# Seven products of halves in place of eight for the gate products of a feed-forward part

## The chip, the core and the metric

One NeuronCore of a Trainium2 chip runs the whole program in one launch. The metric is the time of one execution on the device, in microseconds, as the median of several runs. PE is TensorE (PEld its weight loads), DVE is VectorE, ACT is ScalarE, POOL is GpSimd, and SP issues the DMAs.

## The reference

The input is 512 tokens of width 1024 in float32. Two blocks of a network follow. The second has two layers, and each layer has two feed-forward parts, one ahead of and one behind a token mixer:

```python
def swiglu(x, w_gate, w_up, w_down):
    return (jax.nn.silu(x @ w_gate) * (x @ w_up)) @ w_down
...
for l in range(DEPTH_2):
    h = h + 0.5 * swiglu(rmsnorm_2(h, ffn1_norm[l]), ffn1_w_gate[l], ffn1_w_up[l], ffn1_w_down[l])
    ...
    h = h + 0.5 * swiglu(rmsnorm_2(h, ffn2_norm[l]), ffn2_w_gate[l], ffn2_w_up[l], ffn2_w_down[l])
    gate = jax.nn.sigmoid(rmsnorm_2(h, ple_norm[l]) @ ple_w_gate[l])
    h = h + (p[l] @ ple_w_proj[l]) * gate
```

Here `x` is 512 x 1024, `w_gate` and `w_up` are 1024 x 2816 and `w_down` is 2816 x 1024. The change touches these four feed-forward parts alone.

## The kernel before, in words

Activations lie transposed, features on the 128 partitions and the 512 tokens along the free axis, so a vector of width 1024 is eight tiles of 128 x 512 (`h[k]`, `xh[k]`, `xl[k]`). A float32 product is made of three passes: each operand is split into a high part (ScalarE copies it into the narrower matmul type, L327) and a remainder (VectorE subtracts, L328), and `acc` (L384) issues high x low, low x high and high x high into one PSUM bank.

Weights come in units of 128 x 1024 (four k-tiles of 256 columns, 512 KB). `wunit` (L351) loads a unit on SP's queue into one of three `raw` buffers, and `split` makes `wh` and `wl`, three buffers each. `proj_a` takes 256 columns of a weight at a time: two banks, and for each unit and each half of 128 columns, twelve matmuls of 512 columns. After the last unit it calls the evacuation.

`swiglu_hidden` goes through the 2816 features in 11 pairs of tiles. For each pair it makes the gate products (`evac_g`: VectorE multiplies by the norm's row factors `x.R`, L1203, ScalarE takes Silu, L303) and the up products (`evac_u`: two VectorE multiplications, L1209 and L1210, and a split into `uh` and `ul`), 96 matmuls of 512 columns in all. Then `residual` multiplies all 22 tiles by `w_down`, 256 output columns at a time, and adds half of it to `h` (L1122); in doing so it calls `nxt.add`, which scales and splits `h` for the next part (L330, L331) and sums its squares (L468, L474).

`x.R` is not there when a part starts. `Next.start` puts two steps off by 5 and 8 us of matmul time: the sums over features (L509) and the chain of small VectorE instructions that makes the factors (L530, L521 to L525), and then their broadcast through DRAM (a transpose at L552, a copy at L554, two DMAs). For the first part `between` also rescales `h` by eight VectorE instructions (L1185). Results that come before the factors are held and evacuated after them.

Each engine's queue has an order that is fixed when the program is built. An instruction's rank is its place in the program text (`tc.cur_priority`), and on each engine the ready one of lowest rank goes next by modelled durations; buffers permitting, weights are split up to two units ahead. At run time no queue is reordered by the kernel.

```python
            self.push(self.proj_a(Wg, KD, [(mp * 256, 256)], x.hi, x.lo, evac_g))
            self.push(self.proj_a(Wu, KD, [(mp * 256, 256)], x.hi, x.lo, evac_u))
            self.drain()
        self.push(self.residual(Wd, KF, uh, ul, h, 0.5, nxt=nxt))
```

Of the kernel before, what the change touches and what calls it, by code (L numbers as in the profile page):

```python
# [10 lines left out]
F32 = mybir.dt.float32  # L11
F32R = mybir.dt.float32r
# [65 lines left out]
PASS = 0.2134 / 512  # L78
# [12 lines left out]
KEEP = 2  # L91
EARLY = 3
LATE = 5.0, 8.0
MA, MB, YN = 13, 13, 8
RAW, SPL = 3, 3
AHEAD, EVAC, BEHIND = 1000, -1000, 1000
# [28 lines left out]
class Net:  # L125
# [120 lines left out]
    def nm(self, s):  # L246
        self.n += 1
        return f"{s}{self.n}"

    PLACE = {"h": "H", "mix": "H", "xh": "X", "xl": "X", "mh": "X", "ml": "X", "uh": "U", "ul": "U",  # L250
             "qk": "W", "V": "W", "rc": "W", "hq": "Q", "yh": "Y", "yl": "Y", "oh": "Y", "ol": "Y", "gate": "G"}
    SHORT = ("R", "sq", "g", "u", "hd", "cv", "rows", "out", "lv", "rst", "rt")

    def S(self, name="s", dt=F32):

# [145 lines left out]
    def proj_b(self, W, K, segs, xh, xl, evac):  # L401

        ncol = sum(n for _, n in segs)
        shared = ncol <= 256
        if shared:
            ps = [self.wps() for _ in range(2)]
            ps = [ps[t // 2][:, (t % 2) * 256:(t % 2) * 256 + ncol] for t in range(NT)]
        else:
            ps = [self.wps()[:, :ncol] for _ in range(NT)]
        for k0, nk, (h, l) in self.units(W, K, segs):  # L410
            for t in range(NT):
                for k in range(nk):
# [5 lines left out]
                yield nk * 3 * ncol * PASS  # L418


    def columns(self, parts, dma):
# [30 lines left out]
    class Next:  # L452
# [23 lines left out]
        def start(self, long=True):  # L476
# [711 lines left out]


    def swiglu(self, h, norm, which, l, nxt):  # L1190
        with self.phase({"W": 8}, U=44):
            self.swiglu_hidden(h, norm(), which, l, nxt)

    def swiglu_hidden(self, h, x, which, l, nxt):
        nc, a = self.nc, self.a
        Wg, Wu, Wd = (a[f"{which}_w_{n}_2"][l] for n in ("gate", "up", "down"))
        uh, ul = [], []
        for mp in range(11):
            g = []

            def evac_g(j, p, g=g):
                t = self.S("g")
                nc.vector.tensor_tensor(t, p, x.R, op=OP.mult)  # L1203
                self.act("silu", t, t, AF.Silu)
                g.append(t)

            def evac_u(j, p, g=g):
                u = self.S("u")
                nc.vector.tensor_tensor(u, p, x.R, op=OP.mult)  # L1209
                nc.vector.tensor_tensor(u, u, g[j], op=OP.mult)  # L1210
                hi, lo = self.S("uh", F32R), self.S("ul", F32R)
                self.split(u, hi, lo)
                uh.append(hi)
                ul.append(lo)
            self.push(self.proj_a(Wg, KD, [(mp * 256, 256)], x.hi, x.lo, evac_g))
            self.push(self.proj_a(Wu, KD, [(mp * 256, 256)], x.hi, x.lo, evac_u))
            self.drain()
        self.push(self.residual(Wd, KF, uh, ul, h, 0.5, nxt=nxt))
        self.drain()

    def layer_consts(self):
        t = self.S("layer")
# [636 lines left out]
```

## Time and profile before

| | |
|---|---|
| runs | 3086.03 us median of 3 (3077.51 to 3086.58) |
| profiled execution | 3079.62 us, its span 3077.8 us |
| TensorE matmuls | 14805, 98% of the span busy |
| VectorE, ScalarE, GpSimd | 56%, 38%, 6% of the span busy |
| DMA | 318.69 MB, mean 104 GB/s |

A busy PE in the profile is an engine that has matmuls in flight; how fast it goes is read from the distance between the starts of neighbouring matmuls. PEclk is the granted clock in tenths of full speed.

### The profile page before, as it was taken

Reading aid. Unit: us, or ns where it says so; the run is one execution under the profiler, and the core shown is the slowest. Engines: PE = TensorE matmul, PEld = TensorE weight load, DVE = VectorE, ACT = ScalarE, POOL = GpSimd, SP = SyncE. Lnnn points to the kernel's source line nnn. Section 1 sums busy time; section 2 is a strip of 40 time slices with the busy share of each in tenths; the row PEclk is TensorE's granted clock in tenths of the full one; section 3 lists DMA queues with packets and bytes.
Section 4 is the critical chain, followed back from the end, with each engine's and each line's share of the span. In section 5 each row is a group of like instructions: output and inputs, shape, how many; then the busy total and the mean of one; then the engine's idle time right before and its main releaser. Section 6 shows DMA issues by size and latency. Waiting matters only on the chain.

```text
span 3077.8 us, 37929 instructions
## 1 busy us (share of the span) xinstructions
PE 3011.2 (98%) x14805; PEld 2501.5 (81%) x14805; DVE 1734.0 (56%) x2770; ACT 1159.8 (38%) x1794; POOL 171.1 (6%) x150
## 2 busy tenths in 40 slices
PE   9999999999999999999999999999999999999998
PEld 7778777888888888778888888888888788888888
DVE  5678666666454443587654433644435885644437
ACT  4454534444333322335333322433323353333225
POOL 0000221111000000112000000000000120000000
PEclk9999999999999999999999999999999999999999
DMA  6354324333233333333333333333333224333224
GB/s 206 119 130 131 100 82 129 93 102 96 93 93 110 96 95 97 97 91 86 109 100 96 96 96 99 100 103 96 93 96 106 84 69 126 93 98 98 91 95 152
DMA packets 309061, 318.69 MB, mean 104 GB/s; under 512 B 25230, under 2 KB 284005, under 8 KB 308882
## 3 DMA queue, kind: packets, MB, share of 16 engines
q1 hardware_dynamic: 303502, 307.24, 33.7%
q10 hardware_dynamic: 5380, 9.03, 1.0%
q8 instruction: 116, 1.90, 0.3%
q14 instruction: 63, 0.52, 0.1%
HBM read 289.77 MB, written 7.96 MB: 97 GB/s over the span
## 4 chain that ended last, share of the span: by engine, by line
PE 86%; DVE 7%; issue 3%; DMA 2%; ACT 2%; SPq 1%; POOL 1%; DVEq 0%; ACTq 0%; POOLq 0%
PE w L384 78%; DVE wl L328 2%; PE p L1419 1%; ACT wh L327 1%; PE p L762 1%; PE p L1512 1%; PE p L1580 1%; PE p L723 0%; PE p L769 0%; PE p L509 0%; DMA raw<-in_w_in_dram 0%; PE p L725 0%; PE p L1400 0%; DMA vec<-t5rows 0%; PE p L770 0%
## 5 line engine op out<-in xcount | busy, mean ns | idle before, releaser
L328 DVE TENSOR_TENSOR wl<-raw,wh 128x1024 fp32r<-128x1024 f32 (+3 forms) x524 | 634.6, 1211 | 874.2 <-ACT wh L327 863.1
L384 PE MATMUL w<-xl,wh 128*128 128x512 f32 (+1 forms) x2584 | 1000.9, 387 | 0.0
L384 PE MATMUL w<-xh,wh 128*128 128x512 f32 (+1 forms) x2584 | 998.5, 386 | 0.0
L384 PE MATMUL w<-xh,wl 128*128 128x512 f32 (+1 forms) x2584 | 998.1, 386 | 0.0
L327 ACT ACTIVATE wh<-raw 128x1024 fp32r<-128x1024 f32 (+3 forms) x524 | 537.8, 1026 | 1120.8 <-PE w L384 846.7
L384 PEld LDWEIGHTS w<-xl,wh 128*128 128x128 f32 x2584 | 487.0, 188 | 92.1 <-issue 0.6
L384 PEld LDWEIGHTS w<-xh,wh 128*128 128x128 f32 x2584 | 486.4, 188 | 92.1 <-issue 0.2
L384 PEld LDWEIGHTS w<-xh,wl 128*128 128x128 f32 x2584 | 486.7, 188 | 90.2
L384 PE MATMUL w<-uh,wl 128*128 128x512 f32 x880 | 342.3, 389 | 0.0
L384 PE MATMUL w<-ul,wh 128*128 128x512 f32 x880 | 342.3, 389 | 0.0
L384 PE MATMUL w<-uh,wh 128*128 128x512 f32 x880 | 342.3, 389 | 0.0
L384 PEld LDWEIGHTS w<-uh,wh 128*128 128x128 f32 x880 | 165.2, 188 | 34.4
L384 PEld LDWEIGHTS w<-ul,wh 128*128 128x128 f32 x880 | 165.2, 188 | 34.3
L384 PEld LDWEIGHTS w<-uh,wl 128*128 128x128 f32 x880 | 165.2, 188 | 34.2
L384 PE MATMUL w<-wh,xl 128*128 128x256 f32 (+2 forms) x480 | 141.2, 296 | 2.8 <-ACT wh L327 2.4
L384 PE MATMUL w<-wl,xh 128*128 128x256 f32 (+2 forms) x480 | 139.6, 291 | 0.0
L384 PE MATMUL w<-wh,xh 128*128 128x256 f32 (+2 forms) x480 | 137.8, 291 | 0.0
L1203 DVE TENSOR_TENSOR g<-w,R 128x512 f32<-128x512 f32 x88 | 60.5, 691 | 112.5 <-PE w L384 94.2
L327 ACT ACTIVATE uh<-u 128x512 fp32r<-128x512 f32 x88 | 55.7, 634 | 151.1 <-DVE u L1210 151.1
L303 ACT ACTIVATE g<-g 128x512 f32<-128x512 f32 (+1 forms) x112 | 65.8, 593 | 110.1 <-DVE g L1203 96.7
L384 PEld LDWEIGHTS w<-wh,xl 128*128 128x128 f32 x480 | 92.5, 193 | 7.3 <-ACT wh L327 2.6
L384 PEld LDWEIGHTS w<-wl,xh 128*128 128x128 f32 x480 | 92.8, 193 | 1.5 <-issue 0.7
(394 smaller groups left out, 3222.7 us busy)
## 6 DMA issues: line engine op xcount, KB each, us to landing
raw<-in_ffn_w_gate_dram SPq DMA_DIRECT2D x88, 512.0 KB, 3.8
raw<-in_ffn_w_up_dram SPq DMA_DIRECT2D x88, 512.0 KB, 3.8
raw<-in_ffn_w_down_dram SPq DMA_DIRECT2D x80, 512.0 KB, 3.5
raw<-in_w_in_dram SPq DMA_DIRECT2D x71, 512.0 KB, 3.9
raw<-in_w_up_dram SPq DMA_DIRECT2D x44, 512.0 KB, 3.5
raw<-in_w_gate_dram SPq DMA_DIRECT2D x32, 512.0 KB, 3.5
raw<-in_ple_w_gate_dram SPq DMA_DIRECT2D x24, 512.0 KB, 3.6
raw<-in_w_down_dram SPq DMA_DIRECT2D x20, 512.0 KB, 3.5
```

Of the source, the lines that this page charges most:

```text
L303: self.members.append(self.nc.scalar.activation(*args, **kw).ins)
L327: nc.scalar.activation(hi, src, AF.Copy)
L328: nc.vector.tensor_tensor(lo, src, hi.bitcast(F32), op=OP.subtract)
L384: mm(out, l, r, start=first and i == 0, stop=last and i == 2, skip_group_check=shared)
L762: nc.tensor.transpose(pt[:, i * P:(i + 1) * P], y[:, s * P:(s + 1) * P], self.ident)
L1203: nc.vector.tensor_tensor(t, p, x.R, op=OP.mult)
L1419: nc.tensor.matmul(p[:, t * 64:(t + 1) * 64].rearrange("p (n w) -> p n w", w=w), x[:, t * P:(t + 1) * P], v(x)[:, t * nb:(t + 1) * nb, 1], ...
L1512: nc.tensor.matmul(po[:, t * 64:(t + 1) * 64], sc[s][:, (t - s) * P:(t - s + 1) * P], V[s][:, hv], start=s == 0, stop=s == t)
L1580: nc.tensor.matmul(p[:, :n], q[h][:96, t * P:(t + 1) * P], k[h][:96, :n], start=True, stop=True)
```

## The change

The 40 pairs of feature tiles that are not the first of their part take their gate product by Strassen's scheme. Weights and activations are cut in halves both ways (k-tiles 0 to 3 and 4 to 7; 128 of 256 columns; 256 of 512 tokens), and `seven` makes seven products of 4 k-tiles and 256 tokens in place of eight. Four of them need sums of activation halves, which `half_sums` makes once for each part, behind its first pair in the program; four need differences of weight halves, made for each pair. Two banks hold the results, each of them in two halves, with three additions in PSUM on VectorE and two copies by ScalarE in between. `beside` sets steps of the pair's up product after the third and the fifth of the seven products and behind the last. The hidden features are taken in thirds of 4, 4 and 3 pairs, each followed by its share of `residual`, so `U` shrinks from 44 buffers to 16, and `S`, `B` and `V4` take 36.

```diff
+FF_SLOTS = dict(U=16, S=16, B=16, V4=4)
+THIRDS = (0, 1, 2, 3), (4, 5, 6, 7), (8, 9, 10)
+BESIDE = 0, 0, 1, 0, 1, 0, 0
...
+    def half_sums(self, x):
+        nc, tt = self.nc, self.nc.vector.tensor_tensor
+        out = [([], []) for _ in range(4)]
+        for g in range(2):
+            f = {}
+            for k in (2 * g, 2 * g + 1, 2 * g + 4, 2 * g + 5):
+                f[k] = self.S("uh")
+                tt(f[k], x.hi[k].bitcast(F32), x.lo[k].bitcast(F32), op=OP.add)
+            s = [self.S("uh") for _ in range(4)]
+            for i in range(2):
+                a, b = f[2 * g + i], f[2 * g + i + 4]
+                one, two, c = slice(0, 256), slice(256, 512), slice(256 * i, 256 * i + 256)
+                tt(s[0][:, c], a[:, two], b[:, two], op=OP.add)
+                tt(s[1][:, c], s[0][:, c], a[:, one], op=OP.subtract)
+                tt(s[2][:, c], a[:, one], a[:, two], op=OP.subtract)
+                tt(s[3][:, c], b[:, one], s[1][:, c], op=OP.subtract)
+            for t, (hi, lo) in zip(s, out):
+                h, l = self.S("sxh", F32R), self.S("sxl", F32R)
+                self.split(t, h, l)
+                for y, z in ((hi, h), (lo, l)):
+                    y += [z[:, :256], z[:, 256:]]
+        return out
+
+    def seven(self, W, c0, x, sums, evac):
...
+        for k0 in (0, 4):
+            t = self.rp.tile([P, 1024], F32, name=self.nm("raw"), tag="raw").rearrange("p (k c) -> p k c", k=4)
+            nc.sync.dma_start(t, W[k0 * P:(k0 + 4) * P, c0:c0 + 256].rearrange("(k p) c -> p k c", p=P))
+            raw += [t[:, :, :P], t[:, :, P:]]
+        b11, b12, b21, b22 = raw
+        both = [self.wp.tile([P, 1024], F32R, name=self.nm(n), tag=n) for n in ("wh", "wl")]
...
+        bank, other = self.wps(), self.wps()
+        X, y, z, v = bank[:, one], bank[:, two], other[:, one], other[:, two]
+
+        def product(out, b, a, first=False):
+            for k in range(4):
+                self.acc(out, b[0][:, k], b[1][:, k], a[0][k], a[1][k], first and k == 0, k == 3, shared=True)
+            return 4 * 3 * 256 * PASS
+
+        def keep(p):
+            t = self.S("sv")
+            nc.scalar.activation(t[:, one], p, AF.Copy)
+            return t[:, one]
+        time = product(X, parts(b11, 0), cut(0, one), True)
+        p1 = keep(X)
+        t1 = minus(b12, b11)
+        yield time
+        time = product(z, parts(t1), sums[0], True)
+        p5 = keep(z)
+        t2 = minus(b22, t1)
+        yield time
+        time = product(y, parts(t2), sums[1])
+        tt(y, y, p1, op=OP.add)
+        tt(z, y, p5, op=OP.add)
+        yield time
+        t3, t4 = minus(b22, b12), minus(b21, t2)
+        yield product(X, parts(b21, 1), cut(4, one))
+        time = product(y, parts(t3), sums[2])
+        tt(v, y, p5, op=OP.add)
+        yield time
+        time = product(z, parts(b22), sums[3])
+        evac(1, other)
+        yield time
+        time = product(y, parts(t4), cut(4, two))
+        evac(0, bank)
+        yield time
+
+    def beside(self, long, short, at):
+        for i, t in enumerate(long):
+            yield t
+            for _ in range(at[i]):
+                yield next(short)
+        yield from short
...
-        with self.phase({"W": 8}, U=44):
+        with self.phase({"W": 8}, **FF_SLOTS):
...
+            up = self.proj_a(Wu, KD, [(mp * 256, 256)], x.hi, x.lo, evac_u)
+            if sums is None:
+                yield from self.proj_a(Wg, KD, [(mp * 256, 256)], x.hi, x.lo, evac_g)
+                yield from up
+            else:
+                yield from self.beside(self.seven(Wg, mp * 256, x, sums, evac_g), up, BESIDE)
+        sums = None
+        for third in THIRDS:
+            for mp in third:
+                self.push(work(mp, sums))
+                self.drain()
+                if sums is None:
+                    if self.held:
+                        self.run_late(True)
+                    sums = self.half_sums(x)
+            k = slice(third[0] * 2, third[-1] * 2 + 2)
+            self.push(self.residual(Wd[k.start * P:k.stop * P], k.stop - k.start, uh[k], ul[k], h, 0.5,
+                                    nxt=nxt if third is THIRDS[-1] else None))
             self.drain()
-        self.push(self.residual(Wd, KF, uh, ul, h, 0.5, nxt=nxt))
-        self.drain()
```

`parts` makes a split of 128 x 512 (ScalarE high part, VectorE remainder) and `minus` a VectorE subtraction of 128 x 512.

## Rows read from the trace of the kernel before

**Rows 1.** The page's parts 1 and 2: span, busy time by engine, and the clock that TensorE was granted, in tenths of full speed, in 40 equal slices.
```profile
span 3077.8 us, 37929 instructions
...
PE 3011.2 (98%) x14805; PEld 2501.5 (81%) x14805; DVE 1734.0 (56%) x2770; ACT 1159.8 (38%) x1794; POOL 171.1 (6%) x150
...
PEclk9999999999999999999999999999999999999999
```

**Rows 2.** The page's part 4, the chain of work that ended last, by engine and by line.
```profile
PE 86%; DVE 7%; issue 3%; DMA 2%; ACT 2%; SPq 1%; POOL 1%; DVEq 0%; ACTq 0%; POOLq 0%
PE w L384 78%; DVE wl L328 2%; PE p L1419 1%; ACT wh L327 1%; PE p L762 1%; PE p L1512 1%; PE p L1580 1%; PE p L723 0%; PE p L769 0%; PE p L509 0%; DMA raw<-in_w_in_dram 0%; PE p L725 0%; PE p L1400 0%; DMA vec<-t5rows 0%; PE p L770 0%
```

**Rows 3.** Stretches inside the gate and up products of the first and the second of the four feed-forward parts: length, then busy time and count of PE, PEld, DVE, ACT, POOL, then PEclk, DMA share and GB/s.
```profile
930.00:1130.00 200.00, 200.00 (x884) 165.62 (x883) 91.80 (x109) 61.99 (x74) 0.00 (x0) 1.00 0.33 98
1600.00:1800.00 200.00, 200.00 (x884) 165.62 (x883) 94.57 (x113) 60.74 (x74) 0.00 (x0) 1.00 0.33 98
```

**Rows 4.** TensorE's instructions in order of time, inside gate and up products of 512 columns: the first of 46 matmuls on end and the last (start, us, engine, line, operation).
```profile
1599.68 0.39 PE L384 MATMUL w<-xl,wh 128*128 128x512 f32 x1
...
1609.88 0.39 PE L384 MATMUL w<-xl,wh 128*128 128x512 f32 x1
```

**Rows 5.** The same in the last stage, whose gate products have 256 columns: the first of 85 matmuls on end and the last.
```profile
3019.92 0.28 PE L384 MATMUL w<-xl,wh 128*128 128x256 f32 x1
...
3030.00 0.28 PE L384 MATMUL w<-xl,wh 128*128 128x256 f32 x1
```

**Rows 6.** Weight loads of that stage in order of time.
```profile
3004.63 0.19 PEld L384 LDWEIGHTS w<-xh,wl 128*128 128x128 f32 x1
3004.74 0.19 PEld L384 LDWEIGHTS w<-xh,wh 128*128 128x128 f32 x1
```

**Rows 7.** VectorE's groups by line and shape: count, then busy us, mean ns of one, then idle before.
```profile
L328 DVE TENSOR_TENSOR wl<-raw,wh 128x1024 fp32r<-128x1024 f32 x479 | 599.8, 1252 | 778.0 <-ACT wh L327 766.8 <-DMA rk<-rl 5.3 <-DMA R<-rd 3.9
L1210 DVE TENSOR_TENSOR u<-u,g 128x512 f32<-128x512 f32 x88 | 60.8, 692 | 3.1
L328 DVE TENSOR_TENSOR ul<-u,uh 128x512 fp32r<-128x512 f32 x88 | 60.6, 689 | 32.3 <-ACT uh L327 32.3
...
L1122 DVE SCALAR_TENSOR_TENSOR h<-w,h 128x512 f32<-128x512 f32 x32 | 20.7, 683 | 0.2
...
L1750 DVE TENSOR_TENSOR g<-w,R 128x256 f32<-128x256 f32 x16 | 6.3, 419 | 2.5 <-PE w L384 2.5
```

**Rows 8.** ScalarE's groups by line and shape.
```profile
L327 ACT ACTIVATE wh<-raw 128x1024 fp32r<-128x1024 f32 x479 | 507.1, 1059 | 997.6 <-PE w L384 727.8 <-issue 234.1 <-DMA t5rows<-vec 8.3
...
L327 ACT ACTIVATE uh<-u 128x512 fp32r<-128x512 f32 x88 | 55.7, 634 | 151.1 <-DVE u L1210 151.1
...
L1334 ACT ACTIVATE V<-w,y 128x256 f32<-128x256 f32 x32 | 14.9, 468 | 14.2 <-PE w L384 14.1
```

**Rows 9.** VectorE in order of time, the end of one pair of feature tiles: the evacuation of its second up product and the split of the result (an entry's idle time in brackets).
```profile
960.58 0.68 DVE L1209 TENSOR_TENSOR u<-w,R 128x512 f32<-128x512 f32 x1
...
961.90 1.22 DVE L328 TENSOR_TENSOR wl<-raw,wh 128x1024 fp32r<-128x1024 f32 x1
963.04 0.69 DVE L328 TENSOR_TENSOR ul<-u,uh 128x512 fp32r<-128x512 f32 x1
```

**Rows 10.** The first pair of feature tiles of the first three feed-forward parts, in order, from the first gate matmul on; columns as in rows 3.
```profile
892.14:914.00 21.86, 21.32 (x102) 17.32 (x101) 14.19 (x41) 8.55 (x11) 0.00 (x0) 1.00 0.39 121
1559.16:1581.00 21.84, 21.84 (x102) 18.11 (x101) 11.72 (x24) 7.37 (x10) 0.00 (x0) 1.00 0.31 100
1977.22:1999.00 21.78, 21.41 (x99) 17.47 (x98) 12.47 (x26) 7.89 (x10) 0.00 (x0) 1.00 0.37 109
```

**Rows 11.** The 22 or 23 us ahead of those three points; same columns.
```profile
870.00:892.00 22.00, 22.00 (x99) 18.22 (x98) 4.66 (x6) 3.81 (x4) 0.00 (x0) 1.00 0.33 96
1536.00:1559.00 23.00, 22.03 (x96) 17.93 (x97) 17.60 (x25) 11.48 (x18) 0.00 (x0) 1.00 0.28 74
1955.00:1977.00 22.00, 22.00 (x99) 18.21 (x98) 15.96 (x22) 12.29 (x17) 0.00 (x0) 1.00 0.33 97
```

**Rows 12.** VectorE in order of time at the start of the second part (first gate matmul at 1559.16).
```profile
1562.37 0.75 DVE L331 SCALAR_TENSOR_TENSOR xl<-h,colt,xh 128x512 fp32r<-128x512 f32 x1
1563.03 0.68 DVE L474 TENSOR_TENSOR sq<-sq,sq 128x512 f32<-128x512 f32 x1
1565.59 0.16 DVE L530 TENSOR_SCALAR ms<-p 128x4 f32<-128x4 f32 x1 [1.87 <-PE p L509]
...
1571.30 0.28 DVE L554 COPY rt<-p 4x128 f32<-4x128 f32 x1 [2.54 <-PE p L552]
...
1578.00 1.29 DVE L1203 TENSOR_TENSOR g<-w,R 128x512 f32<-128x512 f32 x2 [4.44 <-DMA R<-rd]
```

**Rows 13.** VectorE in order of time at the start of the first part (first gate matmul at 892.14).
```profile
899.83 0.16 DVE L530 TENSOR_SCALAR ms<-p 128x4 f32<-128x4 f32 x1 [1.44 <-PE p L509]
...
906.11 0.28 DVE L554 COPY rt<-p 8x128 f32<-8x128 f32 x1 [0.36 <-PE p L552]
...
912.42 1.29 DVE L1203 TENSOR_TENSOR g<-w,R 128x512 f32<-128x512 f32 x2 [4.65 <-DMA R<-rd]
913.62 5.39 DVE L1185 SCALAR_TENSOR_TENSOR h<-h,colt,R 128x512 f32<-128x512 f32 x8
```

**Rows 14.** A stretch of the last stage, with products of 256 columns; columns as in rows 3.
```profile
3010.00:3050.00 40.00, 40.00 (x339) 40.00 (x338) 32.59 (x70) 26.97 (x52) 2.87 (x3) 1.00 0.51 165
```

More of the change, by code (lines that the diff above doesn't have):

```diff
@@ L250 @@
     PLACE = {"h": "H", "mix": "H", "xh": "X", "xl": "X", "mh": "X", "ml": "X", "uh": "U", "ul": "U",
+             "sxh": "S", "sxl": "S", "wb": "B", "wt4": "V4",
              "qk": "W", "V": "W", "rc": "W", "hq": "Q", "yh": "Y", "yl": "Y", "oh": "Y", "ol": "Y", "gate": "G"}
-    SHORT = ("R", "sq", "g", "u", "hd", "cv", "rows", "out", "lv", "rst", "rt")
+    SHORT = ("sv", "R", "sq", "g", "u", "hd", "cv", "rows", "out", "lv", "rst", "rt")
     def S(self, name="s", dt=F32):
@@ new lines, in seven, with minus, parts @@
+    def seven(self, W, c0, x, sums, evac):
+        nc, tt = self.nc, self.nc.vector.tensor_tensor
+        raw = []
+        for k0 in (0, 4):
[4 more added lines that the diff above has]
+        both = [self.wp.tile([P, 1024], F32R, name=self.nm(n), tag=n) for n in ("wh", "wl")]
+        four = lambda t: t.rearrange("p (k c) -> p k c", k=4)
+        def minus(a, b):
+            t = four(self.S("wt4"))
+            tt(t, a, b, op=OP.subtract)
+            return t
+        def parts(src, at=None):
+            if at is None:
+                hi, lo = (four(self.S("wb", F32R)) for _ in range(2))
+            else:
+                hi, lo = (four(t[:, at * T:(at + 1) * T]) for t in both)
+            self.split(src, hi, lo)
+            return hi, lo
+        one, two = slice(0, 256), slice(256, 512)
+        cut = lambda k0, c: tuple([t[:, c] for t in y[k0:k0 + 4]] for y in (x.hi, x.lo))
+        bank, other = self.wps(), self.wps()
[31 more added lines that the diff above has]
+        yield time
@@ L1196, in swiglu_hidden, with work, evac_g, evac_u @@
         Wg, Wu, Wd = (a[f"{which}_w_{n}_2"][l] for n in ("gate", "up", "down"))
[L1197 to L1208, printed above, removed]
+        uh, ul = [None] * KF, [None] * KF
+        def work(mp, sums):
+            g = [None] * 2
+            def evac_g(j, p):
+                g[j] = self.S("g")
+                nc.vector.tensor_tensor(g[j], p, x.R, op=OP.mult)
+                self.act("silu", g[j], g[j], AF.Silu)
+            def evac_u(j, p):
+                u, m = self.S("u"), mp * 2 + j
@@ L1209, in evac_u @@
                 nc.vector.tensor_tensor(u, p, x.R, op=OP.mult)
                 nc.vector.tensor_tensor(u, u, g[j], op=OP.mult)
[L1211 to L1216, printed above, removed]
+                uh[m], ul[m] = self.S("uh", F32R), self.S("ul", F32R)
@@ new lines, in evac_u @@
+                self.split(u, uh[m], ul[m])
+            up = self.proj_a(Wu, KD, [(mp * 256, 256)], x.hi, x.lo, evac_u)
+            if sums is None:
+                yield from self.proj_a(Wg, KD, [(mp * 256, 256)], x.hi, x.lo, evac_g)
+                yield from up
+            else:
+                yield from self.beside(self.seven(Wg, mp * 256, x, sums, evac_g), up, BESIDE)
[11 more added lines that the diff above has]
+                                    nxt=nxt if third is THIRDS[-1] else None))
```

## The prediction, made before the kernel was run

> **What bounds the kernel now.** I read the page first: TensorE has matmuls in flight for 98% of the span at the full granted clock [rows 1], and 78% of the chain that ended last lies on the one line that issues matmuls, L384 [rows 2]. Then the stretches of the feed-forward parts: there TensorE is busy without a gap, VectorE 46 to 47% and ScalarE 30 to 31% [rows 3]. So only less TensorE time can help here, and what TensorE costs is read from the distance of starts. 45 steps of 512-column matmuls take 1609.88 - 1599.68 = 10.20 us, **226.7 ns** each [rows 4]; 84 steps of 256-column matmuls take 10.08 us, **120.0 ns** each [rows 5]. Half the columns cost 53%, not half: 13.3 ns of each matmul do not shrink with its columns. The reader should see that this decides how much of the saved eighth is left.
>
> **The products.** A gate product of one pair goes from 2 x 8 x 3 = 48 matmuls of 512 columns to 7 x 4 x 3 = 84 of 256. That is 48 x 226.7 = 10.88 us against 84 x 120.0 = 10.08 us [rows 4, 5]: 0.80 us saved, where the count of columns alone would give an eighth, 1.36. Forty pairs: **32.0 us**. The up and down products keep their matmuls. TensorE had no idle time in these stretches to win back, so 32 is also the most the change can give.
>
> A new weight load stands ahead of each matmul, 36 more in a pair. In the stage with 256 columns the loads last 190 ns and start 110 to 120 ns apart [rows 6], so they overlap each other and the matmuls, and their cost is within the 120.0. The Trainium skill says otherwise (TensorE: Matmul & The Clock Gate, Part 3, The mechanism): a weight load overlaps matmuls in flight only when it uses other row groups, and these loads fill all rows. The trace disagrees, a 190 ns load with a 120.0 ns distance; what that rule would make of the time is a rival below.
>
> **The work on VectorE and ScalarE in a pair.** From its neighbours an instruction of VectorE costs 0.60 us at 512 columns (961.30 to 961.90 is a step of 0.60; a 1024 one takes 1.14, from 961.90 to 963.04) [rows 9], and for 256 columns I take 0.34, the 419 ns of [rows 7] less the overlap of some 0.08 that a 512 one shows (689 against 600). Removed for the gate: two remainders of 1024, 2.3 us. Added: seven remainders and four differences of 512, 6.6 us, and three additions in PSUM, 1.0 us. Net 5.3 us. Before, a pair is 96 x 226.7 = 21.76 us with 94.6 / 9.19 = 10.3 us of VectorE [rows 3]; after, 15.6 in 20.96 us, 74%. ScalarE: two copies of 1.06 go, seven of 0.63 and two kept products of 0.47 come [rows 8]: 6.6 becomes 9.9 us, 47%. Neither is the bound. That TensorE can run unbroken with such neighbours the trace shows in its last stage: VectorE 32.6 of 40 us, TensorE 40 of 40 with 256-column products [rows 14]. The splits and differences hang on weights alone, so they run ahead while buffers last (16 `wb`, of which a pair takes ten), and cost nothing while that lead holds; without it, each would be a wait of about 2 us (difference, copy, remainder).
>
> **The handoffs through PSUM.** Not in the trace, so bounded. Product 3 writes the bank from which ScalarE keeps product 1; product 4 the bank in which VectorE has added; product 6 the bank into which VectorE has written. The covers: product 2 (12 x 120 = 1.44 us), and for the two others a step of the up product (12 x 226.7 = 2.72 us). The chain at its shortest: 0.2 us until the engine starts (an estimate from the gap between a last matmul and its evacuation), 0.47 for ScalarE or 0.76 for VectorE's two, 0.15 back: 0.8 and 1.1 us, both covered. Below: 0. Above: with one 1.06 us copy ahead on ScalarE 1.9 against 1.44, a loss of 0.44; with two 1.2 us remainders ahead on VectorE 3.5 against 2.72, a loss of 0.8; 1.2 us in a pair. As VectorE is free a quarter of the time and the scheduler ranks the older handoff ahead of later splits, I take 0.1 us: **4 us** (0 to 48).
>
> **The start of each part.** This is the costly piece. The half sums are 8 additions of 512, 16 of 256 and 8 remainders of 512: 4.8 + 5.4 + 4.8 = **15.0 us of VectorE**, and 8 x 0.63 = 5 us of ScalarE. They rank behind the whole first pair but ahead of the second pair's splits, so its first product waits for them as well as its second. What VectorE has free in the first pair is 22 less 11.7 to 14.2, some 8 to 10 us [rows 10]: too little for 15. The rest must lie ahead of the first matmul or is a stall, since the up product's weights, which TensorE could do meanwhile, rank behind too.
> - *Second part (and fourth, alike).* Group 0 needs tiles 0, 1, 4, 5 and group 1 the others; the last is written at 1563.1 [rows 12]. Ahead of the gate VectorE has 23 - 17.6 = 5.4 us free [rows 11], room for the four additions of tiles 0 to 3, 2.4; 12.6 are left. Free until the factors land at 1578.0: 1.9 + 2.5 + 6.4 = 10.8 us [rows 12]. Left 1.8 at 1578.0, and older work comes now: gate evacuation 1.2, up evacuation and splits 3.6, then 1.8, then the next pair's first remainder 0.6: 1585.2. TensorE ends the first pair at 1559.16 + 21.76 + 0.9 (sums and transpose) = 1581.8. Stall 3.4, with the second product's chain **4 us**.
> - *First part.* Ahead of it VectorE is free 22 - 4.7 = 17.3 us [rows 11] with tiles 0, 1, 4, 5 long there, so group 0 (7.5) and two additions (1.2) are done; 6.3 are left, against 1.4 + 6.0 us free before the factors at 912.42 [rows 13]. Then 1.2 + 5.3 (L1185) + 3.6 of older work hold the second pair's differences until about 922.6, and product 2 should start at 917.9: **5 us**.
> - *Third part.* The stage ahead has 22 - 16 = 6 us free and its tiles come early [rows 11], and 9.3 more are free in the first pair [rows 10]: **1 us**.
>
> Sum 5 + 4 + 1 + 4 = **14 us**. Bounds: 0, if the sums run ahead wholly; 33, if none of them runs before the gate (5.4 twice, 7.6 and 14.6 by the same ledger).
>
> **The thirds.** `residual` now starts right behind its last pair, three times a part instead of once. Its first unit of four k-tiles, 24 x 226.7 = 5.44 us, covers the last evacuation: from 960.58 to 963.73 is 3.2 us, with a foreign split of 1.14 in it [rows 9], 3.4 from the last matmul. Covered, 0; if it came late by a second split, still under 5.44. There are 16 more additions to `h` in a part, 16 x 0.6 = 10 us of VectorE [rows 7], beside down products in which VectorE is 21% busy [rows 11]. `U` with 16 buffers is full at each third's end; the next third writes into it 20 us after the first of them is free. The number of units and DMAs and the bytes stay; SP issues the same loads, two raw buffers held until the last difference is made, and the lead covers the wait.
>
> **Sum.** 3079.6 (the profiled execution) - 32.0 + 14 + 4 = 3065.6, say **3066 us**. The median of the runs stands 6.4 us above the profiled execution, so against it the gain is what counts: 14 us, 0.45%. 0.3%, 9.3 us, is about what a measurement of this kernel can tell from no change.
>
> **Rivals.**
> 1. *The starts eat the gain.* The half sums stand in VectorE's queue behind everything: stalls of 33 us: 3079.6 - 32 + 33 + 4 = 3085, within 0.3%. For it: 15 us of work and 8 to 10 us of room [rows 10]. Against: 17 us free ahead of the first part [rows 11].
> 2. *VectorE's queue becomes the bound (slower).* A handoff stands behind two splits in an order fixed beforehand, and TensorE waits at product 4 in each pair. At 0.85 us a pair: 3079.6 - 32 + 14 + 34 = 3096. It decides from (32 - 14) / 40 = 0.45 us a pair on. For it: VectorE goes to 74%, and its idle time today ends mostly with ScalarE [rows 7], so waits would chain. Against: [rows 14].
> 3. *All is hidden*: 3079.6 - 32 = 3048. For it: the list of ready work is long; against: the ledger of the second part.
> 4. *Weight loads bind.* If a load excluded matmuls, the 226.7 ns would be 190 of load and 37 of matmul; 256 columns would take 190 + 18 = 208 ns, and a pair 84 x 208 = 17.5 against 10.88 us: 3079.6 + 265 = 3345. Rows 5 and 6 speak against it.
>
> That the products are not those of the scheme would change no time: the instructions are these.
>
> **How the numbers follow.** Forecast 0.53, rival 1 0.20, rival 2 0.14, rival 3 0.12, rival 4 0.01. Faster: 0.85 of the forecast (the rest is stalls 5 us longer) and rival 3, 0.57. Same: 0.13 of the forecast and most of rival 1, 0.24. Slower: rivals 2 and 4 and a rest, 0.19. The range goes from rival 3 to rival 1 and a few us of spread of the runs: 3047 to 3088; it leaves out most of rival 2. The forecast's own range is 3056 to 3075.
>
> **What would show it.** Products of 256 columns at 120 ns in the feed-forward parts, and a pair of 20.96 us in their middle; a longer one names a handoff as the wait of L384. Idle TensorE behind the first pair of each part, 4 to 5 us in parts 1, 2 and 4, ended by a VectorE remainder of a half sum or of the second pair's weights. VectorE at 66% in these parts. No wait where a third's down product starts. The prediction is wrong if the starts cost over 20 us or a pair in the middle more than 21.3.

## The result, and the profile after

The changed kernel takes 3127.39 us (median of 3 runs, 3117.5 to 3127.76) against 3086.03: ratio 1.0132 (95% interval 1.0092 to 1.0173). It is slower by 1.3%, where a gain of 0.45% was forecast and the range ended at 3088. Its profiled execution took 3127.39 us, 47.8 more than that of before; this is the amount to be explained.

The page of the changed kernel, parts 1 and 2, beside [rows 1], then its chain of work that ended last, beside [rows 2]:

```profile
span 3125.6 us, 41947 instructions
...
PE 3007.3 (96%) x16245; PEld 2562.8 (82%) x16245; DVE 2038.3 (65%) x3442; ACT 1282.9 (41%) x2106; POOL 169.2 (5%) x150
...
PEclk9999999999999999999999999999999999999999
...
PE 81%; DVE 10%; issue 3%; DMA 3%; ACT 2%; SPq 0%; POOL 0%; ACTq 0%; DVEq 0%; POOLq 0%
```

TensorE is no longer in flight throughout (96% for 98%), and the chain leaves it more often for VectorE (10% for 7%). Where is not to be seen in rows of 40 slices of 78 us each; that of the clock shows 9 throughout. A stretch of two steady pairs (columns as in [rows 3]) looks just as forecast:

```profile
1622.30:1664.20 41.90, 41.90 (x270) 38.04 (x269) 31.46 (x52) 19.02 (x32) 0.00 (x0) 1.00 0.31 90
```

TensorE is busy for all of it, VectorE 75% (forecast 74%), ScalarE 45% (47%). TensorE in order of time there, the first and the last matmul of product 1 of the third pair, and the first of the fourth pair, which answers to [rows 4, 5]:

```profile
1638.60 0.28 PE L388 MATMUL w<-xl,wh 128*128 128x256 f32 x1
...
1639.91 0.28 PE L388 MATMUL w<-xh,wh 128*128 128x256 f32 x1
...
1659.62 0.28 PE L388 MATMUL w<-xl,wh 128*128 128x256 f32 x1
```

Eleven steps take 1.31 us, 119 ns each, and a pair takes 1659.62 - 1638.60 = 21.02 us where 20.96 were forecast. So the middle is right, and the loss is at the starts. TensorE's waits, by line and releaser (us in total, times, longest), name them:

```profile
PE w L388 <- DVE sxl L332: 34.5, 4, 9.7
...
PE p L652 <- DVE y L625: 7.4, 4, 2.6
PE p L652 <- DVE rr L1279: 5.2, 1, 5.2
...
PE p L823 <- DVE rs L1617: 3.6, 2, 2.4
```

`sxl` is the remainder of a half sum: product 2 of the second pair waits for it once in each part. L652 is the transpose of the row factors (L552 before), which had waited 0.4 us in the first part and nowhere else. TensorE in the second part, in order of time, around both stops (in brackets the idle time and what ended it):

```profile
1590.58 0.39 PE L388 MATMUL w<-xh,wh 128*128 128x512 f32 x1
1593.47 0.27 PE L652 MATMUL p<-ident,y 128*4 128x128 f32 x1 [2.51 <-DVE y L625]
...
1595.12 0.63 PE L388 MATMUL w<-xl,wh 128*128 128x512 f32 x1
1595.55 0.63 PE L388 MATMUL w<-xh,wl 128*128 128x512 f32 x1
...
1607.45 0.28 PE L388 MATMUL w<-xh,wh 128*128 128x256 f32 x1
1615.89 0.58 PE L388 MATMUL w<-sxl,wb 128*128 128x256 f32 x1 [8.15 <-DVE sxl L332]
...
1618.62 0.63 PE L388 MATMUL w<-xl,wh 128*128 128x512 f32 x1
1619.05 0.63 PE L388 MATMUL w<-xh,wl 128*128 128x512 f32 x1
...
1622.30 0.39 PE L388 MATMUL w<-xl,wh 128*128 128x512 f32 x1
1622.53 0.39 PE L388 MATMUL w<-xh,wl 128*128 128x512 f32 x1
```

There is a third cost to be seen here. Behind each of the eight stops of the four parts there are distances of 0.43 us between 512-column matmuls instead of 0.23: 512 columns at 1.2 GHz instead of 2.4. The first pair, with the first stop, and the 21 us behind it, with the second (columns as in [rows 10]; the granted clock is the third number from the end):

```profile
1578.97:1600.80 21.83, 19.32 (x83) 15.58 (x82) 14.78 (x33) 8.74 (x14) 0.00 (x0) 0.92 0.44 124
1600.80:1621.80 21.00, 12.85 (x57) 11.03 (x56) 19.72 (x37) 8.15 (x13) 0.00 (x0) 0.76 0.17 50
```

Taken apart, the granted clock is 1.00 up to 1594.7, 0.51 from 1594.75 to 1598.10, 1.00 from 1598.20 to 1607.70, 0.50 from 1615.89 to 1622.00 and 1.00 again from 1622.30 on: the two slow stretches are at the lower of the two levels.

VectorE in order of time over the same 30 us, which answers to [rows 12]:

```profile
1582.84 0.68 DVE L574 TENSOR_TENSOR sq<-sq,sq 128x512 f32<-128x512 f32 x1
...
1585.43 0.15 DVE L630 TENSOR_SCALAR ms<-p 128x4 f32<-128x4 f32 x1
...
1587.33 0.15 DVE L623 TENSOR_TENSOR nt<-ms,y 128x4 f32<-128x4 f32 x1
1587.40 1.22 DVE L332 TENSOR_TENSOR wl<-raw,wh 128x1024 fp32r<-128x1024 f32 x1
1588.54 0.15 DVE L624 SCALAR_TENSOR_TENSOR nt<-nt,y 128x4 f32<-128x4 f32 x1
1588.61 0.68 DVE L332 TENSOR_TENSOR wb<-wt,wb 128x512 fp32r<-128x512 f32 x1
1589.21 0.15 DVE L625 SCALAR_TENSOR_TENSOR y<-nt,y 128x4 f32<-128x4 f32 x1
...
1593.26 0.15 DVE L625 SCALAR_TENSOR_TENSOR y<-nt,y 128x4 f32<-128x4 f32 x1
1593.78 0.28 DVE L654 COPY rt<-p 4x128 f32<-4x128 f32 x1 [0.36 <-PE p L652]
1599.39 0.69 DVE L464 TENSOR_TENSOR wt<-raw 128x512 f32<-128x512 f32 x1 [5.32 <-DMA raw<-in_ffn_w_gate_dram]
...
1609.45 0.68 DVE L332 TENSOR_TENSOR ul<-u,uh 128x512 fp32r<-128x512 f32 x1
1610.06 2.49 DVE L434 TENSOR_TENSOR uh<-xh,xl 128x512 f32<-128x512 f32 x4
...
1615.15 0.69 DVE L332 TENSOR_TENSOR sxl<-uh,sxh 128x512 fp32r<-128x512 f32 x1
```

Two things are to be seen. In each of the ten gaps between the small steps of the factors' chain stands a remainder or a difference of weights, so the chain lasts from 1585.43 to 1593.4, 8.0 us, and `rt` comes 8.4 us behind `ms` where it came 5.7 behind it in [rows 12], 2.5 of them a wait for a transpose that came in its turn. And the half sums begin at 1610.06, on the heel of the first pair's last `ul`, although all of `xh` and `xl` are there from 1582.9 on and VectorE stands idle for 5.32 us at a stretch. In the other parts it is the same: the last `ul` starts 0.6 us ahead of the first L434.

The account by parts, each counted from its first gate matmul to the end of its last down matmul, in us. "Products" are matmuls by their distances; "slow clock" is the excess of distances over those of the full clock. A stop is counted from start to start, so the matmul ahead of it (0.12 or 0.23 us) is in it and in the products too, 1.2 us in all.

| part | before | after | products before, after | product 2 waits | transpose waits | slow clock |
|---|---|---|---|---|---|---|
| 1 | 361.99 | 374.42 | 358.99, 350.98 | 10.0 | 5.6 | 4.8 |
| 2 | 360.12 | 368.49 | 358.99, 350.98 | 8.4 | 2.9 | 4.7 |
| 3 | 360.74 | 367.57 | 358.99, 350.98 | 8.3 | 2.6 | 3.4 |
| 4 | 360.12 | 369.12 | 358.99, 350.98 | 8.9 | 3.0 | 3.8 |
| sum | 1443.0 | 1479.6 | 1436.0, 1403.9 | 35.6 | 14.1 (0.8 before) | 16.6 (0.7 before) |

The products gain 32.0; the stops and the clock behind them take 35.6 + 13.3 + 15.9 = 64.8, less the 1.2 counted twice, and other short gaps about 5. That is +36.6 (1479.6 - 1443.0). The other 11.2 us lie outside the four parts, in the two token mixers (313.45 for 305.03, and 309.88 for 306.55 us), whose instructions are the same in another order.

### The profile page after: what moved, and what is told of

Same layout as the page of the kernel before. It is cut to its first block, busy times and chain, and to the rows that moved or that the text cites. A ratio compares the mean times of both kernels' runs of the same rounds, so it can differ in the third digit from the quotient of the medians.

```text
span 3125.6 us, 41947 instructions
## 1 busy us (share of the span) xinstructions
PE 3007.3 (96%) x16245; PEld 2562.8 (82%) x16245; DVE 2038.3 (65%) x3442; ACT 1282.9 (41%) x2106; POOL 169.2 (5%) x150
## 4 chain that ended last, share of the span: by engine, by line
PE 81%; DVE 10%; issue 3%; DMA 3%; ACT 2%; SPq 0%; POOL 0%; ACTq 0%; DVEq 0%; POOLq 0%
PE w L388 73%; DVE wl L332 2%; PE p L1531 1%; ACT wh L331 1%; PE p L862 1%; PE p L1624 1%; PE p L1692 1%; PE p L823 0%; PE p L869 0%; PE p L825 0%; DVE uh L434 0%; DMA raw<-in_ffn_w_gate_dram 0%; PE p L609 0%; DVE wb L332 0%; PE p L1512 0%
## 5 line engine op out<-in xcount | busy, mean ns | idle before, releaser
L388 PE MATMUL w<-xl,wh 128*128 128x512 f32 (+1 forms) x2264 | 849.4, 375 | 0.1
L388 PE MATMUL w<-xh,wl 128*128 128x512 f32 (+1 forms) x2264 | 845.3, 373 | 0.0
L388 PE MATMUL w<-xh,wh 128*128 128x512 f32 (+1 forms) x2264 | 844.0, 373 | 0.0
L388 PEld LDWEIGHTS w<-xl,wh 128*128 128x128 f32 x2264 | 431.4, 191 | 68.7 <-DVE w L498 1.2
L388 PEld LDWEIGHTS w<-xh,wh 128*128 128x128 f32 x2264 | 430.1, 190 | 69.0 <-issue 0.2
L388 PE MATMUL w<-sxh,wb 128*128 128x256 f32 x1280 | 240.0, 286 | 0.0
L388 PE MATMUL w<-sxl,wb 128*128 128x256 f32 x640 | 184.1, 288 | 35.1 <-DVE sxl L332 34.5
L388 PEld LDWEIGHTS w<-sxh,wb 128*128 128x128 f32 x1280 | 202.9, 195 | 1.7
L388 PEld LDWEIGHTS w<-sxl,wb 128*128 128x128 f32 x640 | 124.6, 195 | 39.2 <-DVE sxl L332 35.9
L331 ACT ACTIVATE wb<-wt 128x512 fp32r<-128x512 f32 x160 | 100.3, 629 | 132.0 <-DVE wt L464 128.6
```

The costliest lines, as they stand in the source:

```text
L331: nc.scalar.activation(hi, src, AF.Copy)
L388: mm(out, l, r, start=first and i == 0, stop=last and i == 2, skip_group_check=shared)
```

## The experiments

Two theories. **A**: the half sums are late because of where their scratch tiles live. They are named `uh`, so they come out of `U`, whose buffers are given out in the order of the program; the first pair's `uh` and `ul` come first, and those hang on the row factors. **B**: the transpose is late because the fixed order puts other work into each gap of the chain of small instructions, and TensorE's queue stops behind it. The rivals are that VectorE simply has too much to do there, that the thirds or the handoffs cost it, and that a wait taken away comes back at the next place. Ratios are to the kernel before, run beside on the same chip.

**e1_tag**: the scratch tiles from the weights' buffers.

```diff
-                f[k] = self.S("uh")
+                f[k] = self.S("wb")
-            s = [self.S("uh") for _ in range(4)]
+            s = [self.S("wb") for _ in range(4)]
```

> The half sums' sixteen scratch tiles taken from pool B (where the weight pieces lie) and not from pool U, nothing else. Theory A, buffers of one pool are handed out in the order of the program, so the half sums, which ask for U behind the first pair, cannot start before that pair's last remainder (ul) has its U buffer: the sums move into the first pair, the wait of 8.3 to 10.0 us of product 2 shrinks to the 1 to 5 us of the ledger in each part and most of the half-clock stretch behind it goes, 30 to 40 us less than the changed kernel. Theory B, VectorE has no room for the sums in the first pair whatever the buffers: the four waits stay at 8 us or more, and the time within 5 us of the changed kernel's. By both, the chain that makes the row factors stays as long as it is (another foreign instruction in each of its gaps), so the 2.5 to 5.6 us in front of the factors' transpose stay.

Measured 3083.89 us, ratio 1.0008 (0.9999 to 1.0018), where the changed kernel had 1.0132: two names give back some 40 us. VectorE in the second part (first gate matmul at 1563.25):

```profile
1567.72 2.49 DVE L434 TENSOR_TENSOR wb<-xh,xl 128x512 f32<-128x512 f32 x4
```

The sums begin 4.5 us into the part instead of 31.1. Product 2 waits 0.8 us at most. TensorE's waits show what is left:

```profile
PE w L388 <- DVE wl L332: 10.6, 5, 3.5
PE p L652 <- DVE rr L1279: 8.0, 1, 8.0
```

The sums now stand ahead of the second pair's own splits, whose product 1 waits 3.4, 3.7 and 3.4 us in parts 2 to 4, and they make the first part's chain longer still. The expectation missed the transposes: in parts 2 to 4 they wait 0.4 us at most, and 8.0 in the first. So A holds, and the rival "it comes back at the next place" holds for a smaller part.

**e2_later**: second pair with eight products, the sums first used in the third.

```diff
-                self.push(work(mp, sums))
+                self.push(work(mp, sums if mp > 1 else None))
```

> The second pair of each part takes its gate product the old way too; the half sums stay where they are in the program and in pool U, and are first needed by the third pair, 21.8 us later. Theory A: they still start behind the first pair's last ul, but have the second pair for cover: the four waits (35.6 us) and their half-clock stretches (some 10 us) go, 4 x 0.8 = 3.2 us of saving are given up: 40 to 45 us less than the changed kernel, about the time of before. Theory B: VectorE is behind by 15 us and stays behind, so half or more of the wait shows up at the third pair, 20 us less at most. The wait in front of the factors' transpose stays by both.

Measured 3087.06 us, ratio 1.0020 (1.0010 to 1.0029); parts 366.3, 361.4, 361.7, 361.1. The sums stand where they stood in rank, ahead of the second pair's splits, and TensorE waits for those splits: 23.5 us on `wl` for the whole run. A later use alone takes back most of the loss and wins nothing over the kernel before; the rank has to move too. One thing was not expected: no transpose of the parts waits over 0.5 us. The second pair's eight products bring a single remainder into the gaps of the factors' chain, as in the kernel before, so it is the splits and differences of the seven that stretch it.

**e3_thirds**: thirds and the small `U`, no sums and no seven products.

```diff
-            if sums is None:
+            if True:
-                    sums = self.half_sums(x)
+                    sums = ()
```

> The features in thirds with the small U pool, all gate products the old way, no half sums. Theory A: no loss in the feed-forward parts (360 to 362 us each as before), the transpose not late. The 11 us that the changed kernel lost outside these parts (8 and 3 us in the two mixers): if the thirds or the new pool sizes shift the mixers' order, they show here as +8 to +11 us against before; if they come from the seven products' other load, this run is within 3 us of before.

Measured 3082.74 us, ratio 1.0000 (0.9989 to 1.0011); parts 362.1, 360.1, 360.7, 360.1, those of before to 0.1 us. The thirds cost nothing.

**e4_nosums**: the seven products take slices of `x` where the sums belong, so the work of the sums is left out (and the buffers `S`, which nothing uses then).

```diff
-                    sums = self.half_sums(x)
+                    half = lambda k0, c: tuple([t[:, c] for t in y[k0:k0 + 4]] for y in (x.hi, x.lo))
+                    one, two = slice(0, 256), slice(256, 512)
+                    sums = half(0, two), half(4, one), half(0, one), half(4, two)
```

> The half sums are left out: slices of the activations stand in their place, so the gate products are not the reference's. All seven products, weight differences, additions in PSUM and thirds stay. If the starts are the whole of the loss, the four waits of product 2 and the half-clock stretches behind them go, 40 to 48 us less than the changed kernel, and the 14 us in front of the transposes stay, since weight pieces run into the gaps of the chain: within 5 us of before. If the steady pairs lose something that the trace hides, it stays above before by over 10 us.

Measured 3075.98 us, ratio 0.9983 (0.9974 to 0.9992); parts 362.3, 355.9, 357.3, 357.0. The 35.6 us at product 2 are gone. The transposes still wait, so those waits are not the sums' doing:

```profile
PE p L652 <- DVE y L625: 7.1, 3, 2.5
PE p L652 <- DVE rr L1279: 5.2, 1, 5.2
```

**e5_pow**: the factors' reciprocal root by one GpSimd power instead of ten VectorE instructions, in the changed kernel. **b_pow**: the same in the kernel before.

```diff
-POW, MP = 2, 0
+POW, MP = 4, 0
```

> The changed kernel with one constant other: the reciprocal square root of the row factors is one GpSimd power instead of ten small VectorE instructions, wherever the program has one for four columns. Theory B (the waits of TensorE at the transpose of the factors, 5.6 + 2.9 + 2.6 + 3.0 = 14.0 us in the four parts, come from foreign instructions that go into the gaps of the chain of small VectorE instructions): with the chain gone these waits fall below 1 us each, about 3 us in all, so -11, and of the 16.6 us at half clock the part that follows these stops goes too, about -5; the wait of the second product for the half sums (35.6) stays. Changed kernel less 16: about 3111, ratio to the kernel before 1.008. Rival (the transpose waits for something else, such as the sums of squares or the order of TensorE's own queue): waits unchanged, ratio 1.013.

> Control: the kernel before with the same one constant other. In its four parts TensorE waits 0.8 us at these transposes, so Theory B has nothing to win there: ratio 0.998 to 1.001, parts of 360 to 362 us as before. Rival (the power on GpSimd is worth something by itself, wherever factors are made): ratio under 0.997; then what the variants with it give must be read against this kernel and not against the kernel before.

e5_pow: 3113.23 us, ratio 1.0097 (1.0077 to 1.0117); parts 371.1, 363.9, 366.4, 367.5. b_pow: 3085.38, ratio 1.0011 (1.0002 to 1.0021), parts as before. With the chain gone no transpose of the parts waits as long as 0.5 us, which is B. The expected 1.008 lies in the interval, but not all of the account is as expected: the wait of product 2, which was to stay, grew:

```profile
PE w L388 <- DVE sxl L332: 43.8, 4, 14.9
```

The two stops lie one behind the other on TensorE, and the sums come behind the last `ul` still; the earlier TensorE arrives at product 2, the longer it waits there (45.0 us for 35.6 in the account).

**e6_late**: instead, the transpose is put off from 8 to 17.5 us of matmul time in these parts. **b_late**: the same in the kernel before.

```diff
+FF_LATE = 5.0, 17.5
...
-            self.swiglu_hidden(h, norm(), which, l, nxt)
+            global LATE
+            own, LATE = LATE, FF_LATE
+            x = norm()
+            LATE = own
+            self.swiglu_hidden(h, x, which, l, nxt)
```

> The changed kernel with the factors' transpose put off from 8 to 17.5 us of matmul time in the four parts, and nothing else: the scratch tiles of the half sums stand where the change put them, among the buffers of the hidden features. Theory A (these buffers are handed out in program order, so the sums start only behind the first pair's last remainder, and that hangs on the factors): the waits at the transpose go (14.0), but the factors land some 3 us later than in the changed kernel, and TensorE, which lost nothing at the transpose, stands at the second product earlier, so the wait for the sums grows by about 3 + 3 us in a part, from 35.6 to about 60: ratio 1.013 to 1.018, no better than the changed kernel. Rival (what c3_tag_late gained over e1_tag comes from the later transpose whatever the sums' buffers): about 15 below the changed kernel, ratio 1.008.

> Control: the kernel before with the transpose of the factors put off as in c3_tag_late. TensorE waits 0.8 us there at present: ratio 0.999 to 1.001, parts of 360 to 362 us. Rival (the later transpose is worth something by itself): ratio under 0.997, and c3_tag_late's gain is not the seven products'.

e6_late: 3130.5 us, ratio 1.0156 (1.0141 to 1.0172). b_late: 3083.47, ratio 0.9999 (0.9989 to 1.0009). No transpose stops TensorE for as much as 0.5 us, and product 2 waits 19.7 + 15.8 + 14.3 + 16.3 = 66.1 us. VectorE in the second part of e6_late:

```profile
1607.48 1.28 DVE L333 TENSOR_TENSOR ul<-u,uh 128x512 fp32r<-128x512 f32 x2
1608.68 2.49 DVE L435 TENSOR_TENSOR uh<-xh,xl 128x512 f32<-128x512 f32 x4
```

This is the plainest evidence for A: make the factors later, and the sums, which do not use them, go with the last `ul` again. In the four runs in which the scratch tiles are named `uh` (the changed kernel, e2_later, e5_pow, e6_late) the first sum starts 0.6 us behind the start of the last `ul` in all 16 parts. `U` was not full then, by the code: the first pair has taken 4 of its 16 buffers.

**c1_tag_pow**: e1_tag and the power together.

```diff
-POW, MP = 2, 0
+POW, MP = 4, 0
...
-                f[k] = self.S("uh")
+                f[k] = self.S("wb")
```

> The half sums' scratch tiles out of the weights' buffers (as in e1_tag) and the power on GpSimd. Theories A and B together: of e1_tag the first part's wait of 8.4 us at the transpose goes, and some 1 to 2 us of half clock: 1441.7 - 9 = 1433 for the four parts; the waits at the third pair's first product (3.4, 3.7, 3.4) stay, since they come behind the sums' remainders. About 10 below the kernel before: ratio 0.9965 to 0.998. Rival (taking one wait away only moves it to the next handoff, as e1_tag did): first part still 365, ratio 1.000.

Measured 3095.5 us, ratio 1.0042 (1.0029 to 1.0055), a miss. (What the expectation calls the third pair's first product is the second's, as in e1_tag.) The first part has 365.7 us as in e1_tag, which the rival had said. VectorE there, with the second pair's product 1 waiting 9.2 us from 919.33 to 928.56:

```profile
916.32 5.37 DVE L1285 SCALAR_TENSOR_TENSOR h<-h,colt,R 128x512 f32<-128x512 f32 x8
...
927.83 0.67 DVE L332 TENSOR_TENSOR wl<-raw,wh 128x512 fp32r<-128x512 f32 x1
```

The earlier factors bring the rescaling of `h` and the first pair's evacuations earlier, and these now stand between the sums. Parts 2 to 4 did not gain (359.1, 360.6, 359.3), and 7.3 us of its excess over e1_tag's profiled execution lie outside the parts, 3.4 of them in the first mixer, where the power costs something by itself: that mixer takes 308.0 to 309.2 us in the three runs with the power and 304.3 to 306.7 in the nine without.

**c3_tag_late**: e1_tag and the later transpose together.

```diff
+FF_LATE = 5.0, 17.5
...
-                f[k] = self.S("uh")
+                f[k] = self.S("wb")
```

> As e1_tag, with the chain of small instructions as it was, but the transpose of the factors put off from 8 to 17.5 us of matmul time in these four parts, so that in TensorE's queue it stands behind most of the first pair. Theory B: the stretched chain (about 14 us behind the first matmul) is done by then, the waits at the transpose go as in c1_tag_pow (-9 in the first part, -0.6 in the others), but the factors land some 9 us later and the evacuations of the first pair with them, behind which nothing of TensorE waits before the banks run out: ratio 0.997 to 0.999. Rival (the banks held for the factors bind, or the late evacuations fall among the splits of the second and third pair): new waits of 2 us or more in the second or third pair of each part, ratio 1.000 to 1.004.

Measured 3068.55 us, ratio 0.9957 (0.9942 to 0.9972); parts 365.2, 353.7, 356.2, 353.9, where e1_tag has 365.1, 358.7, 359.3, 358.6. The edit that made the changed kernel no better gives 15 us once the sums no longer hang on the factors, more than expected and not in the way expected: the first part, whose wait at the transpose goes, gains nothing, and the gain lies in parts 2 to 4, where the transposes of e1_tag had waited 0.4 us at most. There it is the wait of product 1 (3.4 to 3.7 us) that goes. The factors land later, so the first pair's evacuations (`g`) no longer stand ahead of the remainder `wl` that product 1 waits for. VectorE in the second part of e1_tag and of c3_tag_late:

```profile
1581.10 1.27 DVE L1304 TENSOR_TENSOR g<-w,R 128x512 f32<-128x512 f32 x2
...
1589.10 0.68 DVE L332 TENSOR_TENSOR wl<-raw,wh 128x512 fp32r<-128x512 f32 x1
```

```profile
1581.70 0.68 DVE L333 TENSOR_TENSOR wl<-raw,wh 128x512 fp32r<-128x512 f32 x1
...
1588.45 1.27 DVE L1309 TENSOR_TENSOR g<-w,R 128x512 f32<-128x512 f32 x2
```

With the first gate matmuls at 1563.25 and 1562.10, `wl` starts 25.9 us into the part in the one and 19.6 in the other. In parts 2 to 4 TensorE's gaps come to 0.5, 3.8 and 1.1 us. The first part still loses 9.5 in products 2 and 3 of the second pair. VectorE there, and in its place in time the matmul with the longest wait:

```profile
919.57 0.67 DVE L1309 TENSOR_TENSOR g<-w,R 128x512 f32<-128x512 f32 x1
920.17 5.37 DVE L1286 SCALAR_TENSOR_TENSOR h<-h,colt,R 128x512 f32<-128x512 f32 x8
925.47 0.67 DVE L1309 TENSOR_TENSOR g<-w,R 128x512 f32<-128x512 f32 x1
927.27 0.58 PE L389 MATMUL w<-sxl,wb 128*128 128x256 f32 x1 [6.00 <-ACT sv L487]
928.47 0.67 DVE L333 TENSOR_TENSOR wb<-wt,wb 128x512 fp32r<-128x512 f32 x1
```

The remainder at 928.47 stands behind the rescaling of `h`. The 6.0 us are no wait for a remainder, though, as the expectation of d2_first has it: product 3 waits for ScalarE to keep product 1 (`sv`, at 926.83), and in ScalarE's order that copy stands behind the Silu of the second `g`, which VectorE makes behind the rescaling (925.47). So a handoff does cost time where VectorE is late.

**d2_first**: c3_tag_late, and in the first part alone the second pair keeps its eight products, with the sums ranked behind its splits. **d3_both**: the rescaling ranked later as well (the last edit below).

```diff
-                self.push(work(mp, sums))
+                first = which == "ffn1" and l == 0
+                self.push(work(mp, None if first and mp < 2 else sums))
...
+                    own = self.tc.cur_priority
+                    self.tc.cur_priority += 120 if first else 0
                     sums = self.half_sums(x)
+                    self.tc.cur_priority = own
...
+            own = self.tc.cur_priority
+            self.tc.cur_priority += 300
             for k, t in enumerate(h):
                 nc.vector.scalar_tensor_tensor(t, t, self.col("norm_final_g", k), R1, op0=OP.mult, op1=OP.mult)
+            self.tc.cur_priority = own
```

> As c3_tag_late, but in the first of the four parts alone the second pair keeps its eight products and the half sums are ranked behind that pair's weights, so that the seven products begin with the third pair there. In c3_tag_late this part has 365.2 us, 9.5 of them waits of the second pair's second and third product for remainders that stand behind the rescaling of h (5.4 us) and the first pair's evacuations. Theory: those waits go for 0.8 us of products: first part 355 to 357, the others as in c3_tag_late, ratio 0.992 to 0.9945. Rival (as in e2_later, the second pair's own weights then stand behind that VectorE work, and the wait only changes its name): first part 362 or more, ratio 0.995 or above.

> As d2_first, with the rescaling of h (eight VectorE instructions, 5.4 us, in the first part) ranked behind the work of the next pairs as well. If d2_first has a wait of up to 5 us left in the first part's second or third pair, ended by a remainder behind the rescaling, it goes: ratio 0.991 to 0.993. If it has none, the time is d2_first's within 2 us. Rival: the rescaling is late for the first down products, which add to h, and TensorE waits there.

d2_first: 3058.27 us, ratio 0.9921 (0.9906 to 0.9935); parts 356.0, 354.0, 355.7, 353.5, together 1419.2. d3_both: 3058.05, ratio 0.9921, so nothing was left for the second edit. Both beat the kernel before by 0.8%. Busy time in d2_first, from its page, and then what is left of TensorE's waits for `wl`, which were 23.5 us in e2_later:

```profile
PE 2985.0 (98%) x16209; PEld 2544.3 (83%) x16209; DVE 2028.5 (66%) x3430; ACT 1279.2 (42%) x2099; POOL 170.4 (6%) x150
```

```profile
PE w L389 <- DVE wl L333: 2.1, 3, 1.2
```

23.8 of the 32.0 us of products come through in the four parts (1443.0 - 1419.2; one pair less saves 0.8 less). VectorE does nearly the same work as in the changed kernel (2028.5 us busy for 2038.3), all the half sums included, so the amount of work was not the cause.

## Why the prediction was wrong, by its own steps

- **What bounds the kernel, and the products**: right. The distances of [rows 4, 5] held in the new place, the account has 32.0 us, and weight loads of 195 ns overlap as in [rows 6]. Rival 4 falls.
- **Work in a pair**: right, 75% of VectorE for 74, and no wait over 0.5 us in the steady pairs.
- **Handoffs**: 4 us forecast. In the whole changed kernel the waits for kept products and added banks come to 0.5 us ahead of matmuls and 2.6 us ahead of weight loads, which run beside matmuls; a pair in the middle costs 0.06 over its products. They cost nearly nothing while VectorE is on time (6.0 us once in c3_tag_late, where it was not). Rival 2, the one on the slower side, falls.
- **Thirds, SP and DMA**: 0 forecast, 0 measured (e3_thirds).
- **The start of each part**: this step failed. It forecast 14 us with 33 as the upper bound; measured are some 64, and 5 of short gaps. Its ledger took the half sums as work that goes into any free time of VectorE as soon as its inputs are there. The fixed order did not allow it: the scratch tiles of the sums come behind the first pair's `uh` and `ul` in `U` (e1_tag, e6_late), so none of VectorE's idle time, 7.0 us in the first pair of the second part, went to the sums. The upper bound was wrong in the same way: "none of them runs before the gate" is not the worst case, "none of them runs before the first pair is evacuated" is. That alone is 35.6 us. Product 1 of the second pair, which the forecast let wait for the sums as well, did not: with the sums held back its splits ran first.
- Two terms **were missing**. The prediction put the sums into the idle time around the chain of factors without asking who waits for the chain: TensorE's queue does, at the transpose, and its wait grew by 13.3 us (it goes in e5_pow and e6_late). The chain was stretched by the splits and differences of the second pair's seven products, not by the sums: e4_nosums has the same waits, e2_later none. And a stop was counted at its own length, where [rows 10] show TensorE at its full clock; behind each stop it ran at the lower one, 15.9 us more, a third on top of the stops.
- **Rival 1** named the place and not the size. "The starts cost over 20 us" was set down as what would make the prediction wrong, and so it was.
- **Open**: the 11.2 us in the mixers. In the first, where the excess is 8.4, TensorE has a new wait of 2.4 us for `rs` (L1617) and one of 1.2 for a DMA, and the granted clock is 0.93 in the last 74 us, where it had been 1.00. None of the twelve runs was made to tell what in the order does it; with the same code there, that mixer takes 304.3 to 306.7 us in the nine runs without the power, e6_late among them, which differs from the changed kernel in the time of the transpose alone. The 3.3 of the second mixer may be chance: it takes 303.7 to 310.7 us in the same nine, and executions of the kernel before alone range from 3075.6 to 3089.0 us.

## What to carry to other kernels

When work is moved into the idle time of an engine, look up what lets it start: not only its inputs, but the pool that its scratch tiles come from, and who is ahead of them there. A scratch tile takes the place in the queue of the pool that it is named into. And when a free engine is filled, look at the chains of small steps on it that another engine's queue waits for: put that queue's instruction later, which cost nothing in the kernel before (b_late). Look again after each step: here a later transpose gained by what it moved on VectorE, not by the wait it was meant for (c3_tag_late).

## What was not expected of the hardware

The price of a stop does not end with it. Behind the one of 2.9 us (1590.58 to 1593.47) the distances of 512-column matmuls stayed at 0.23 us for another 1.3 us and then were 0.43 until 1598.11; behind the one of 8.4 us they were long from the first matmul on. In the kernel before, whose stops in these parts are under 1 us, the granted clock is 1.00 in all four parts; the 0.7 us of its column are single distances of 0.32 us behind small matmuls. The Trainium skill (TensorE: Matmul & The Clock Gate, Part 1, What's actually happening) describes a clock that is set to one of two levels by how busy TensorE has been; the trace agrees, with a granted clock of 1.00 or about 0.5, in these parts the lower one behind stops alone.

At the lower level the 13.3 ns that do not shrink with the columns are not there: 512 columns start 427 ns apart (1618.62 to 1619.05 in two decimals), which is 512/1.2, while at the full level they take 226.7 ns and not 512/2.4 = 213. The same page of the Trainium skill (Part 1, Wait — 56ns, not 53.3ns?) has N/1.2 at the lower level too, but only 2.5 ns over N/2.4 at the full one; for these matmuls, each with a weight load of its own, the traces have 13.3.
